# The Fourier gate of a hybrid encoder by Strassen's seven products

## The chip, the cores and the metric

The kernel runs on one core of a Trainium2 chip. The metric is device time of one execution in microseconds (us). The engines are TensorE (PE, matrix products and transposes), VectorE (DVE), ScalarE (ACT), GpSimd (POOL) and SyncE (SP); all data between HBM and SBUF moves by DMAs, which SP, ACT or POOL issue from their own instruction queues. Each engine takes its instructions in order.

## The reference, cut to what matters

Two token streams, 2048 prompt tokens and 512 sample tokens of 1024 channels, go through an attention layer, a Fourier layer and a final RMSNorm. Only the Fourier layer is touched:

```python
def fourier_layer(x, g, w_gate, w_out):
    h = rmsnorm(x, g)
    hg = h.astype(jnp.float32).reshape(b, s, N_FGROUPS, FGROUP_CH)   # 4 groups of 256 channels
    f = jnp.fft.fftn(hg, axes=(1, 3), norm="ortho").real.reshape(b, s, d)
    gate = h @ w_gate                                                # (tokens, 1024) @ (1024, 1024)
    return x + (f * jax.nn.silu(gate)) @ w_out
```

The gate product `h @ w_gate` is what the change rewrites.

## The kernel before, in words

The 2560 tokens are 20 tiles of 128: tiles 0 to 15 of the prompt and 16 to 19 of the sample. Every fp32 product is made as three fp32r matmuls by `matmul3` (L80): high part by high, high by low, low by high. So every operand is first split: ACT casts it to the high part, DVE (or POOL) subtracts that from the source for the low part.

`attention_phase` does the attention layer and writes its result to HBM as `x1d`. Its last out-projection is left over as a list of steps, `tail`. `fourier_phase(tail)` (L560) runs those steps with its own first work laid between them.

The Fourier layer runs in two stages. In the first, each token tile is loaded and normalised (`norm_T` L620: DMA of `x` L623, Square with a sum on ACT L617, L76 on DVE, a power on POOL L77, the scaling on DVE L625), transposed by PE in two halves of four 128x128 blocks (L602), and split (`split_T` L595: ACT L608, DVE L609). From the transposed halves come two products. `channel_dft` (L628) makes z, the DFT along the channels: 24 matmuls of 128x256. `gate` (L641) makes the gate: two output halves, each 8 blocks of the contraction by three matmuls, 48 of 128x512 to a tile; then tanh on ACT (L647), the product on DVE (L648) and a store to `s2d`. `w_gate` is loaded once by `load_res` (L576) in eight steps of 512 KB (`w32g`) and held, split, in 16 tiles of `wres`.

The tiles run in five groups: the sample's four, then the prompt's tiles a, a+4, a+8, a+12 for a = 0 to 3. After each group `radix4` (L655) makes sums and differences of its four z tiles on DVE; for the prompt the odd parts go to HBM (`odd`) and the even parts stay in SBUF. The norm of a tile is issued one tile ahead, and the gate of a tile lags z by one tile, in the last group by three (`pend`). So at the end three gates are left (`last_gates`); they run half by half after the first `position` work, and `load_res` of `w_fout` follows, in the tiles that the gate's weights leave.

In the second stage `position` (L714) makes the DFT along the tokens, multiplies with the gate from `s2d`, and `finish` (L766) makes the out-projection (`fo`), the residual and the final norm.

At the seam of the two phases the loop L674 to L707 matters: `tail` holds the steps of the last out-projection (`op`, residual `xr` added on DVE L475, stored to `x1d`); norms of tiles 16 and 17 are issued after steps 4 and 6, with their loads on ACT's queue, and a step of `load_res` follows each step from the third on. The order within each engine is then made by the framework's scheduler from this program order and the dependencies; buffers in pools of fixed size (here `wres` 16, `x` 3, `s2` 3, `Z` 14, `xr` 3, `hT` 8, PSUM `bank` 6 and `acc` 2) make a writer wait until the former tenant is read.

Of the kernel before, what the change touches and what calls it, by code (L numbers as in the profile page):

```python
# [18 lines left out]
P = 128  # L19
# [12 lines left out]
LINE = 512  # L32
LATE = (0, 8, 9, 10, 11, 12)
# [9 lines left out]
def encoder(  # L43
# [36 lines left out]
    def matmul3(out, a, b, start, stop, w=None):  # L80

        PE.matmul(out, a[0], b[0], start=start, stop=False)  # L82
        PE.matmul(out, a[0], b[1], start=False, stop=False)  # L83
        PE.matmul(out, a[1], b[0], start=False, stop=stop)  # L84
# [475 lines left out]
    def fourier_phase(tail):  # L560
        with ExitStack() as es:
# [4 lines left out]
            SP.dma_start(gb, bass.AP(g1.tensor, g1.offset, [[0, P], [1, D]]))  # L566

            mir = fp.tile([P, 120], I32, name="mir")[:, :8]
            SP.dma_start(mir, mirror)
            ch = fp.tile([P, 2, 2, 256], F32R, tag="tab", bufs=2, name="chan_sb")  # L570
            POOL.dma_start(ch, chan)

            def zt(name):
                return zp.tile([P, D], F32, tag="Z", bufs=14, name=name)

            def load_res(w, name, stage):  # L576

                res, steps = [], []

                def load(half, k2):  # L580
                    w32 = stage(f"w32{name}{half}_{k2}")
                    SP.dma_start(w32, w[half, k2])
                    for kk in range(2):
                        t = fp.tile([P, 2, 512], F32R, align_bytes=LINE, tag="wres", bufs=16, name=f"wr{name}{half}_{k2}_{kk}")
# [35 lines left out]
            def norm_T(t, queue=SP):  # L620

                xt = fp.tile([P, D], F32, tag="x", bufs=3, name=f"x1_{t}")
                queue.dma_start(xt, x1d[t * P : (t + 1) * P, :])  # L623
                inv = sumsq(xt, f"b{t}")
                DVE.scalar_tensor_tensor(xt, xt, inv[:, 0:1], gb, ALU.mult, ALU.mult)  # L625
                return split_T(xt, f"b{t}")

            def channel_dft(t, hT, zscale):  # L628
                z = zt(f"z{t}")
                for hf in range(2):  # L630
                    ps = bank(f"z{t}_{hf}")
                    for gg in range(2):
                        for kk in range(2):
                            matmul3(
                                ps[:, gg * 256 : gg * 256 + 256], hT[hf * 4 + gg * 2 + kk],
                                (ch[:, kk, 0], ch[:, kk, 1]), kk == 0, kk == 1,
                            )
                    ACT.activation(z[:, hf * 512 : hf * 512 + 512], ps, AF.Copy, scale=zscale)
                return z

            def gate(t, hT, halves=(0, 1)):  # L641
                for half in halves:
                    ps = psum2.tile([P, 512], F32, tag="acc", name=f"gp{t}_{half}")
                    for k in range(KD):
                        matmul3(ps, hT[k], wg[half * KD + k], k == 0, k == KD - 1)
                    th = main.tile([P, 512], F32, tag="xr", bufs=3, name=f"gt{t}_{half}")
                    ACT.activation(th, ps, AF.Tanh, scale=0.5)  # L647
                    DVE.scalar_tensor_tensor(th, th, 1.0, ps, ALU.add, ALU.mult)  # L648
# [6 lines left out]
            def radix4(z, name):  # L655

                e, f = zt(f"e{name}"), zt(f"f{name}")
                tt(e, z[0], z[2], ALU.add)
                tt(z[0], z[0], z[2], ALU.subtract)
                tt(f, z[1], z[3], ALU.add)  # L660
                tt(z[1], z[1], z[3], ALU.subtract)
                w2 = zt(f"w{name}")
                tt(w2, e, f, ALU.subtract)
                tt(e, e, f, ALU.add)
                return e, w2, z[0], z[1]


            def s2_tile(name):
                return fp.tile([P, D], F32, tag="s2", bufs=3, name=name)

            def x_tile(name):
                return fp.tile([P, D], F32, tag="x", bufs=3, name=name)
# [41 lines left out]
            def position(name, tab, gr, gs, tiles):  # L714
# [11 lines left out]
                tb = fp.tile([P, 6, P], F32R, tag="tab", bufs=2, name=f"tb{name}")  # L726
# [4 lines left out]
                us = [zp.tile([P, D], F32, tag="u", bufs=2, name=f"u{name}_{i}") for i in range(len(tiles))]  # L731
# [34 lines left out]
            def finish(uT, r, last=False):  # L766
# [3 lines left out]
                if last:  # L770
                    ss = main.tile([P, 8], F32, tag="ss", bufs=2, name="ssl")
                    junk = fp.tile([P, D], BF16, tag="junk", bufs=1, name="jkl")
                x2 = fp.tile([P, D], F32, tag="x", bufs=3, name=f"x2_{r0}")
# [27 lines left out]
            last_gates, pend = pend, []  # L801
# [30 lines left out]
            w0, w2 = ([parts[a][i] for a in range(4)] for i in range(2))  # L832
# [158 lines left out]
```

## Time and profile before

| | |
|---|---|
| time, median of 3 runs | 1725.6 us (1723.79 to 1727.31) |
| profiled execution | 1727.91 us, span 1726.1 us, mean granted clock 0.989 |
| PE busy | 1681.3 us, 97% of the span |
| PE weight loads | 1442.8 us, 84% |
| DVE, ACT, POOL busy | 1119.8, 811.2 and 308.0 us |
| DMA | 306.92 MB, 178 GB/s on average |

The attention phase takes up to about 1124 us of the span, the Fourier layer's first stage (with the last half of the out-projection) from there to about 1452, the second stage the rest. Times in a timeline count from the span's start. A matmul is pipelined: its shown duration overlaps that of the next, so the distance between starts is what one costs. `[2.42 <-DVE x L625]` behind a line is idle time of that engine before the instruction and what ended it.

### The profile page before, as it was taken

The numbers are of one execution on the slowest core, as the hardware profiler recorded it, in microseconds if no ns is written. First come the engines' busy times: TensorE is split into PE (matmuls) and PEld (weight loads), VectorE is DVE, ScalarE is ACT, GpSimd is POOL, SyncE is SP. The second block draws the span as 40 slices with busy tenths as digits, with TensorE's granted clock in tenths as the row PEclk, the third lists the DMA queues.
The fourth block names the chain that finished last, engine by engine and source line by source line (L and its number), as shares of the span: only waits on it lengthen the run. The fifth ranks groups of instructions, "written<-read, shape, count | busy, mean of one in ns | idle before, by whom it ended". The sixth has DMA issues, their size and how long they took to land. (4 is left out here: it accounts for less than half of the span.)

```text
span 1726.1 us, 25388 instructions
## 1 busy us (share of the span) xinstructions
PE 1681.3 (97%) x9100; PEld 1442.8 (84%) x9100; DVE 1119.8 (65%) x2696; ACT 811.2 (47%) x1864; POOL 308.0 (18%) x395
## 2 busy tenths in 40 slices
PE   9999899999989999899999999989999999999998
PEld 7878778888888888888888888878888888888886
DVE  5898655888438885378874688655344348597553
ACT  6677524676226664256652466443332224343221
POOL 2467640111301112101121011100000000011100
PEclk9999899999999999999999999999999999999999
DMA  8478775444574454743538534484322347443421
GB/s 298 165 284 322 265 277 183 160 172 167 201 253 138 155 183 159 269 156 135 203 121 285 209 125 141 144 285 136 108 89 94 109 138 262 161 141 120 143 95 62
DMA packets 83450, 306.92 MB, mean 178 GB/s; under 512 B 9931, under 2 KB 20171, under 8 KB 65404
## 3 DMA queue, kind: packets, MB, share of 16 engines
q1 hardware_dynamic: 75836, 265.18, 45.0%
q0 software_dynamic: 7056, 38.80, 5.7%
q8 instruction: 73, 1.20, 0.3%
q10 hardware_dynamic: 432, 1.31, 0.3%
q14 instruction: 53, 0.43, 0.1%
HBM read 238.11 MB, written 67.14 MB: 177 GB/s over the span
## 5 line engine op out<-in xcount | busy, mean ns | idle before, releaser
L400 ACT ACTIVATE S<-S 128x385 f32<-128x385 f32 (+1 forms) x320 | 191.2, 598 | 53.7 <-DVE S L396 52.7
L417 ACT CAST pts<-pt 128x384 fp32r<-128x384 f32 (+1 forms) x320 | 144.8, 454 | 117.7 <-PE pt L416 113.0
L418 DVE TENSOR_TENSOR pts<-pt,pts 128x384 fp32r<-128x384 f32 (+1 forms) x320 | 168.5, 527 | 42.6 <-ACT pts L417 39.8
L396 DVE CUSTOM_DVE_ANT_0 S<-spt,b 128x385 f32<-128x385 f32 (+1 forms) x320 | 168.8, 528 | 34.2 <-PE spt L384 29.1
L445 POOL TENSOR_TENSOR o<-o,s 128x256 f32<-128x256 f32 x75 | 55.4, 739 | 692.7 <-DVE o L441 686.3
L384 PE MATMUL spt<-kwin,qab 128*128 128x384 f32 (+1 forms) x640 | 159.1, 330 | 8.9 <-DVE S L396 8.9
L405 DVE TENSOR_SCALAR S<-S 128x384 f32<-128x384 f32 (+1 forms) x320 | 149.4, 467 | 9.1
L416 PE MATMUL pt<-ident,S 128*128 128x128 f32 x896 | 150.7, 274 | 0.6 <-DVE pts L418 0.4
L384 PEld LDWEIGHTS spt<-kwin,qab 128*128 128x128 f32 x640 | 118.6, 189 | 37.9 <-DVE S L396 12.6
L82 PE MATMUL gp<-h,wg 128*128 128x512 f32 x320 | 137.7, 430 | 0.0
L82 PE MATMUL qp<-h,wq 128*128 128x512 f32 x320 | 137.1, 429 | 0.6 <-ACT wq L96 0.6
L430 PEld LDWEIGHTS av<-pts,v 128*128 128x128 f32 x896 | 126.6, 190 | 11.5 <-DVE pts L418 0.2
L430 PE MATMUL av<-pts,v 128*128 128x256 f32 x896 | 135.2, 285 | 0.0
L82 PE MATMUL op<-wo,uT 128*128 128x512 f32 x320 | 127.6, 401 | 3.5 <-DVE xr L475 2.8
L416 PEld LDWEIGHTS pt<-ident,S 128*128 128x128 f32 x896 | 114.2, 141 | 16.1 <-DVE pts L418 4.3
L83 PE MATMUL op<-wo,uT 128*128 128x512 f32 x320 | 127.1, 397 | 0.0
L84 PE MATMUL op<-wo,uT 128*128 128x512 f32 x320 | 126.4, 396 | 0.0
L84 PE MATMUL qp<-h,wq 128*128 128x512 f32 x320 | 126.1, 394 | 0.1
L84 PE MATMUL gp<-h,wg 128*128 128x512 f32 x320 | 126.0, 394 | 0.0
L83 PE MATMUL qp<-h,wq 128*128 128x512 f32 x320 | 125.6, 393 | 0.0
L82 PE MATMUL fo<-wrf,tTu 128*128 128x512 f32 x320 | 125.6, 392 | 0.0
L83 PE MATMUL gp<-h,wg 128*128 128x512 f32 x320 | 125.5, 392 | 0.0
(270 smaller groups left out, 3941.7 us busy)
## 6 DMA issues: line engine op xcount, KB each, us to landing
wq<-wsd SPq DMA_DIRECT2D x32, 1024.0 KB, 4.9
wg<-wsd SPq DMA_DIRECT2D x32, 1024.0 KB, 6.7
wo<-wsd SPq DMA_DIRECT2D x32, 1024.0 KB, 4.9
x<-x1d SPq DMA_DIRECT2D x38, 512.0 KB, 3.9
b<-rowd SPq DMA_DIRECT2D x40, 384.0 KB, 4.2
xs<-in_x_dram SPq DMA_DIRECT2D x23, 512.0 KB, 7.4
xr<-in_x_dram SPq DMA_DIRECT2D x40, 256.0 KB, 5.5
x1d<-xr SPq DMA_DIRECT2D x40, 256.0 KB, 4.0
```

The source lines that it names most:

```text
L82: PE.matmul(out, a[0], b[0], start=start, stop=False)
L83: PE.matmul(out, a[0], b[1], start=False, stop=False)
L84: PE.matmul(out, a[1], b[0], start=False, stop=stop)
L384: PE.matmul(ps[:, 2 + k0 * P : 2 + k1 * P], q, kwin[g][:, part, b * P + k0 * P : b * P + k1 * P], start=part == 0, stop=part == 1,)
L396: DVE.tensor_tensor_reduce(out=s[:, e0:e1], in0=ps[:, 1 + e0 : 1 + e1], in1=st["bias"][:, j, 386 - e1 : 386 - e0][:, ::-1], scale=1.0, sca ...
L400: last_exp[0] = ACT.activation(s[:, e0:e1], s[:, e0:e1], AF.Exp, bias=mn, scale=-1.0, accum_out=den)
L405: DVE.tensor_scalar(s[:, ks], s[:, ks], den, None, ALU.mult)
L416: PE.transpose(ps[:, kb, :], s[:, 1 + kb * P : 1 + (kb + 1) * P], ident)
L417: ACT.copy(hi[:, k0:k1, j, :], ps[:, k0:k1, :])
L418: DVE.tensor_tensor(lo[:, k0:k1, j, :], ps[:, k0:k1, :], f32(hi[:, k0:k1, j, :]), ALU.subtract)
L430: PE.matmul(out, v, pt[:, kb].rearrange("p h q -> p (h q)"), start=kb == k0 and part == 0, stop=kb == k1 - 1 and part == 1,)
L445: eng.tensor_tensor(of, of, res["s"][:, cs], ALU.mult)
```

## The change

The gate product now takes two token tiles at once, as a 2 by 2 block product: the rows of A are the two tiles (0 and 1), its columns the halves of the contraction, and B is `w_gate` in quadrants. Strassen's algorithm, in Winograd's form, needs seven products of blocks instead of eight:

- sums of A: S1 = A21 + A22, S2 = S1 - A11, S3 = A11 - A21, S4 = A12 - S2, made on DVE (with ACT copies) from the transposed halves in PSUM for each pair and split like any operand (`sums`, `parts`);
- sums of B: T1 = B12 - B11, T2 = B22 - T1, T3 = B22 - B12, N4 = B21 - T2, made once and split (`build1`, `build2`);
- products: W = A11 B11, X = A12 B21, Z = S1 T1, W += S2 T2, Z += S4 B22, W += S3 T3, W += A22 N4, with ACT and DVE taking W and Z out of PSUM in between; C11 = A11 B11 + X, C12 and C22 are sums of such copies, C21 is the last W.

Each product is 4 blocks by three matmuls of 128x512, so a pair takes 84 instead of 96. Six weight sets (B11, T1, T2, B22, T3, N4) are held in SBUF; the split B21 is written to HBM (`b21d`) and loaded again for each pair in four DMAs of 512 KB on SP. `build1(k)` is laid between the tail's steps where `load_res` was; `build2(k)` reads `w_gate` a second time, after pair 0's transposes. The work of the next pair (transposes, sums, z, and the radix-4 sums of every second pair) is laid between the products by hooks. The pools become two: `L` with 24 slots of 4 KB to a partition, and `R` with 16, which hold almost everything, so that `c`, `x`, `s2`, staged weights and sums share slots. The scratch of Square moves to the three `xr` buffers, which silu tiles and the out-projection's residuals also use. The even parts of `radix4` go to HBM (`evd`) and come back before the second stage's prompt part. At the end the last pair's gates run whole, with `position` of the sample laid in after the first product, and `w_fout` is loaded after them.

In the changed file lines 80 to 560 are shifted by one: L602 of before answers to L662 there, L625 to L639, L609 to L665.

```diff
+def left(shape, dtype, name):
+    return fp.tile(shape, dtype, align_bytes=LINE, tag="L", bufs=24, name=name)
+def right(shape, dtype, name):
+    return zp.tile(shape, dtype, align_bytes=LINE, tag="R", bufs=16, name=name)
+ch = left([P, 2, 2, 256], F32R, "chan_sb")
...
+def split(t, src, lo_engine=DVE):
+    ACT.copy(t[:, 0], src)
+    lo_engine.tensor_tensor(t[:, 1], src, f32(t[:, 0]), ALU.subtract)
+    return t[:, 0], t[:, 1]
...
-    junk = fp.tile([P, D], BF16, tag="junk", bufs=1, name=f"jk{name}")
+    junk = main.tile([P, 512], F32, tag="xr", bufs=3, name=f"jk{name}").bitcast(BF16)
     ACT.activation(junk, src, AF.Square, accum_out=ss[:, 0:1])
     return inv_rms(ss, 1, f"inv{name}")
...
+class Pair:
+    def __init__(self, n, ts):
+        self.n, self.ts, self.x, self.ps, self.A, self.F, self.S = n, ts, [None, None], {}, {}, {}, {}
+        self.zs = [None, None]
+    def norms(self, i, queue=SP):
+        self.x[i] = norm(self.ts[i], queue)
+    def turn(self, i, hf):
+        name = f"b{self.ts[i]}_{hf}"
+        ps = bank(f"tr{name}")
+        for k in range(4):
+            c0 = (hf * 4 + k) * P
+            PE.transpose(ps[:, k * P : (k + 1) * P], self.x[i][:, c0 : c0 + P], ident)
+        t = main.tile([P, 2, 512], F32R, align_bytes=LINE, tag="hT", bufs=8, name=f"tT{name}")
+        ACT.copy(t[:, 0], ps)
+        DVE.tensor_tensor(t[:, 1], ps, f32(t[:, 0]), ALU.subtract)
+        self.ps[i, hf], self.A[i, hf] = ps, (t[:, 0], t[:, 1])
+    def sums(self, i):
+        ps, F = self.ps, self.F
+        if i in (1, 4):
+            self.pair = left([P, 2, 512], F32, f"s{i}_{self.n}")
+        out = F[i] = self.pair[:, i in (2, 3)]
+        if i % 2:
+            ACT.copy(out, ps[1, 0])
+        a, b, op = {
+            1: lambda: (out, ps[1, 1], ALU.add),
+            2: lambda: (F[1], ps[0, 0], ALU.subtract),
+            3: lambda: (ps[0, 0], out, ALU.subtract),
+            4: lambda: (ps[0, 1], F[2], ALU.subtract),
+        }[i]()
+        DVE.tensor_tensor(out, a, b, op)
+    def parts(self, i):
+        self.S[i] = split(left([P, 2, 512], F32R, f"S{i}_{self.n}"), self.F[i])
...
+def prod(out, a, b, ks, first):
+    for k in ks:
+        cs = slice(k * P, (k + 1) * P)
+        matmul3(out, (a[0][:, cs], a[1][:, cs]), b[k], first and k == 0, k == 3, not first)
+def gates(pr, hooks):
+    n, A, S = pr.n, pr.A, pr.S
+    W = psum2.tile([P, 512], F32, tag="acc", name=f"W{n}")
+    Z = psum2.tile([P, 512], F32, tag="acc", name=f"Z{n}")
+    X = bank(f"X{n}")
+    b21 = []
+    def more():
+        if len(b21) < 4:
+            t = right([P, 2, 512], F32R, f"b21_{n}_{len(b21)}")
+            SP.dma_start(f32(t), f32(b21d[len(b21)]))
+            b21.append((t[:, 0], t[:, 1]))
+    def x_step(k):
+        prod(X, A[0, 1], b21, (k,), True)
+        more()
+    def silu(c, i, half):
+        th = main.tile([P, 512], F32, tag="xr", bufs=3, name=f"gt{pr.ts[i]}_{half}")
+        ACT.activation(th, c, AF.Tanh, scale=0.5)
+        DVE.scalar_tensor_tensor(th, th, 1.0, c, ALU.add, ALU.mult)
+        t = pr.ts[i]
         dst, t0 = (s2d[0], t) if t < SEQ // P else (s2d[1], t - SEQ // P)
         SP.dma_start(dst[t0 * P : (t0 + 1) * P, half * 512 : half * 512 + 512], th)
+    def hook(i):
+        for h in hooks.get(i, ()):
+            h()
+    more()
+    more()
+    four = range(4)
+    c = left([P, 2, 512], F32, f"c{n}")
+    c11, c22 = c[:, 0], c[:, 1]
+    prod(W, A[0, 0], wg["B11"], four, True)
+    ACT.copy(c11, W)
+    hook(0)
+    x_step(0)
+    prod(Z, S[1], wg["T1"], four, True)
+    ACT.copy(c22, Z)
+    hook(1)
+    prod(W, S[2], wg["T2"], four, False)
+    c12 = fp.tile([P, 512], F32, tag="c12", bufs=1, name=f"c12_{n}")
+    ACT.copy(c12, W)
+    hook(2)
+    x_step(1)
+    prod(Z, S[4], wg["B22"], four, False)
+    DVE.tensor_tensor(c12, c12, Z, ALU.add)
+    silu(c12, 0, 1)
+    hook(3)
+    x_step(2)
+    prod(W, S[3], wg["T3"], four, False)
+    DVE.tensor_tensor(c22, c22, W, ALU.add)
+    silu(c22, 1, 1)
+    hook(4)
+    x_step(3)
+    DVE.tensor_tensor(c11, c11, X, ALU.add)
+    silu(c11, 0, 0)
+    hook(5)
+    prod(W, A[1, 1], wg["N4"], four, False)
+    silu(W, 1, 0)
+    hook(6)
+b21d = [dram.tile([P, 2, 512], F32R, name=f"b21d{k}") for k in range(4)]
+wg = {w: [None] * 4 for w in ("B11", "T1", "T2", "B22", "T3", "N4")}
+def stage_w(w, k, name):
+    rows = []
+    for r in (k, k + 4):
+        t = left([P, 2, 512], F32, f"w32{name}{r}")
+        SP.dma_start(t, w[:, r // 2, :, (r % 2) * 512 : (r % 2) * 512 + 512].rearrange("h p c -> p h c"))
+        rows.append(t)
+    return rows[0][:, 0], rows[0][:, 1], rows[1][:, 0], rows[1][:, 1]
+def build1(k):
+    def w(name):
+        return left([P, 2, 512], F32R, f"w{name}_{k}")
+    b11, b12, b21, b22 = stage_w(w_gate, k, "g")
+    wg["B11"][k] = split(w("B11"), b11)
+    DVE.tensor_tensor(b12, b12, b11, ALU.subtract)
+    wg["T1"][k] = split(w("T1"), b12)
+    DVE.tensor_tensor(b11, b22, b12, ALU.subtract)
+    wg["T2"][k] = split(w("T2"), b11)
+    wg["B22"][k] = split(w("B22"), b22, POOL)
+    t = w("B21")
+    split(t, b21, POOL)
+    POOL.dma_start(f32(b21d[k]), f32(t))
+def build2(k):
+    def w(name):
+        return right([P, 2, 512], F32R, f"w{name}_{k}")
+    b11, b12, b21, b22 = stage_w(w_gate, k, "h")
+    DVE.tensor_tensor(b22, b22, b12, ALU.subtract)
+    DVE.tensor_tensor(b21, b21, b11, ALU.subtract)
+    DVE.tensor_tensor(b21, b21, b22, ALU.subtract)
+    wg["T3"][k] = split(w("T3"), b22)
+    wg["N4"][k] = split(w("N4"), b21, POOL)
...
 order = [[16, 17, 18, 19]] + [[a, a + 4, a + 8, a + 12] for a in range(4)]
-ahead = []
-wg, loads = load_res(w_gate, "g", s2_tile)
+pairs = [Pair(2 * gi + i // 2, tiles[i : i + 2]) for gi, tiles in enumerate(order) for i in (0, 2)]
+builds = [lambda k=k: build1(k) for k in range(4)]
 for i, s in enumerate(tail):
     s()
     if i in (4, 6):
-        ahead.append(norm_T(order[0][len(ahead)], ACT))
-    if i >= 2 and loads:
-        loads.pop(0)()
-for s in loads:
-    s()
+        pairs[0].norms((i - 4) // 2, ACT)
+    if i % 2 and builds:
+        builds.pop(0)()
 wstack.close()
 zp = es.enter_context(tc.tile_pool(name="zp", bufs=1, side="right", reuse_waits="tile"))
-todo = [t for tiles in order for t in tiles][2:]
-parts = []
-pend = []
-for gi, tiles in enumerate(order):
-    zs = []
-    for t in tiles:
-        hT = ahead.pop(0)
-        if todo:
-            ahead.append(norm_T(todo.pop(0)))
-        zs.append(channel_dft(t, hT, 1.0 if gi == 0 else 0.5))
-        pend.append((t, hT))
-        if len(pend) > (3 if gi == 4 else 1):
-            gate(*pend.pop(0))
-    r = radix4(zs, f"r{gi}")
-    if gi == 0:
-        for i in range(4):
-            SP.dma_start(gsd[i], r[i])
-    else:
-        parts.append(r[:2])
-        for i in range(2):
-            SP.dma_start(odd[gi - 1, i], r[2 + i])
+def turns1(pr):
+    pr.turn(1, 0)
+    pr.turn(1, 1)
+    pr.sums(1)
+def turns2(pr):
+    pr.turn(0, 0)
+    pr.sums(2)
+    pr.parts(1)
+    pr.turn(0, 1)
+    pr.sums(4)
+    pr.parts(2)
+def turns3(pr):
+    pr.parts(4)
+def turns4(pr):
+    pr.sums(3)
+    pr.parts(3)
+def combine(pr):
+    if pr.n % 2 == 0:
+        return
+    gi = pr.n // 2
+    r = radix4(pairs[pr.n - 1].zs + pr.zs, f"r{gi}")
+    for i in range(4):
+        SP.dma_start(gsd[i] if gi == 0 else evd[gi - 1, i] if i < 2 else odd[gi - 1, i - 2], r[i])
+evd = dram.tile([4, 2, P, D], F32, name="evd")
+pr = pairs[0]
+for f in (turns1, turns2, turns3, turns4):
+    f(pr)
+build2(0)
+build2(1)
+for i, hf in HALVES:
+    pr.z(i, hf)
+build2(2)
+build2(3)
+for n, pr in enumerate(pairs[:-1]):
+    nx = pairs[n + 1]
+    for i in range(2):
+        nx.norms(1 - i)
+    gates(pr, {
+        1: [lambda: turns1(nx)], 2: [lambda: turns2(nx)], 3: [lambda: turns3(nx)], 4: [lambda: turns4(nx)],
+        5: [lambda: nx.z(1, 0), lambda: nx.z(1, 1)],
+        6: [lambda: nx.z(0, 0), lambda: nx.z(0, 1), lambda: combine(nx)],
+    })
...
-first = position(*sample(1, (2, 3)))
-for half in range(2):
-    for t, hT in last_gates:
-        gate(t, hT, (half,))
+first = []
+gates(pairs[-1], {0: [lambda: first.extend(position(*sample(1, (2, 3))))]})
...
-w0, w2 = ([parts[a][i] for a in range(4)] for i in range(2))
+w0, w2 = [], []
+for i, l in enumerate((w0, w2)):
+    for a in range(4):
+        t = zt(f"ev{a}_{i}")
+        SP.dma_start(t, evd[a, i])
+        l.append(t)
```

More of the change, by code (lines that the diff above doesn't have):

```diff
@@ L32 @@
 LINE = 512
+HALVES = ((1, 0), (1, 1), (0, 0), (0, 1))
 LATE = (0, 8, 9, 10, 11, 12)
@@ L78, in inv_rms, with matmul3 @@
         return inv
[L80 to L84, printed above, removed]
+    def matmul3(out, a, b, start, stop, more=False):
+        PE.matmul(out, a[0], b[0], start=start, stop=False, skip_group_check=more)
+        PE.matmul(out, a[0], b[1], start=False, stop=False, skip_group_check=more)
+        PE.matmul(out, a[1], b[0], start=False, stop=stop, skip_group_check=more)
     def load_w(c, n, name, lo_engine=None, late=None):
@@ L583, in load @@
                     for kk in range(2):
-                        t = fp.tile([P, 2, 512], F32R, align_bytes=LINE, tag="wres", bufs=16, name=f"wr{name}{half}_{k2}_{kk}")
+                        t = left([P, 2, 512], F32R, f"wr{name}{half}_{k2}_{kk}")
                         src = w32[:, kk * 512 : kk * 512 + 512]
@@ L615, in sumsq, with norm @@
                 ss = main.tile([P, 8], F32, tag="ss", bufs=2, name=f"ss{name}")
-                junk = fp.tile([P, D], BF16, tag="junk", bufs=1, name=f"jk{name}")
+                junk = main.tile([P, 512], F32, tag="xr", bufs=3, name=f"jk{name}").bitcast(BF16)
                 ACT.activation(junk, src, AF.Square, accum_out=ss[:, 0:1])
                 return inv_rms(ss, 1, f"inv{name}")
-            def norm_T(t, queue=SP):
-                xt = fp.tile([P, D], F32, tag="x", bufs=3, name=f"x1_{t}")
+            def norm(t, queue=SP):
+                xt = left([P, D], F32, f"x1_{t}")
                 queue.dma_start(xt, x1d[t * P : (t + 1) * P, :])
@@ L625, in norm_T, with z @@
                 DVE.scalar_tensor_tensor(xt, xt, inv[:, 0:1], gb, ALU.mult, ALU.mult)
[L626 to L630, printed above, removed]
+                return xt
+            class Pair:
[30 more added lines that the diff above has]
+                    self.S[i] = split(left([P, 2, 512], F32R, f"S{i}_{self.n}"), self.F[i])
+                def z(self, i, hf):
+                    t = self.ts[i]
+                    if hf == 0:
+                        self.zs[i] = zt(f"z{t}")
@@ L637, in channel_dft @@
                             )
[L638 to L648, printed above, removed]
+                    ACT.activation(
+                        self.zs[i][:, hf * 512 : hf * 512 + 512], ps, AF.Copy, scale=1.0 if t >= SEQ // P else 0.5
+                    )
@@ L725, in position @@
                     s2s.append(s2)
-                tb = fp.tile([P, 6, P], F32R, tag="tab", bufs=2, name=f"tb{name}")
+                tb = left([P, 6, P], F32R, f"tb{name}")
                 POOL.dma_start(tb.rearrange("p a c -> p (a c)"), tabs[tab])
@@ L730, in position @@
                 asb = main.tile([P, 4, P], F32, tag="xr", bufs=3, name=f"as{name}")
-                us = [zp.tile([P, D], F32, tag="u", bufs=2, name=f"u{name}_{i}") for i in range(len(tiles))]
+                us = [zt(f"u{name}_{i}") for i in range(len(tiles))]
                 for hf in range(2):
```

30 lines of the change are left out of this document (15 added, 15 removed).

## The prediction

> **What bounds the kernel now.** I read the page's first lines, then a table of stretches across the stage that is changed, the waits of TensorE (PE) where the stage begins, PE's timeline there, and last the rows by shape that price what is added.
>
> ```profile
> span 1726.1 us, 25388 instructions
> PE 1681.3 (97%) x9100; PEld 1442.8 (84%) x9100; DVE 1119.8 (65%) x2696; ACT 811.2 (47%) x1864; POOL 308.0 (18%) x395
> ```
>
> PE is busy for 97% of the span, so the kernel ends when PE's work ends. All times below are of this one profiled execution, 1727.91 us (span 1726.1, and 1.8 around it); it lies 2.3 above the median of 1725.6 and 0.6 above the highest of the three runs. About 0.2% (3.5 us) is what a measurement of this kernel can tell from no change.
>
> ```profile
> 1123.00:1165.00 42.00, 36.67 (x166) 29.90 (x166) 24.05 (x39) 18.26 (x33) 2.20 (x4) 0.92 0.85 291
> 1165.00:1200.00 35.00, 35.00 (x205) 30.93 (x204) 19.98 (x27) 14.49 (x27) 3.55 (x5) 0.99 0.39 125
> 1200.00:1260.00 60.00, 60.00 (x328) 51.98 (x327) 23.12 (x31) 18.04 (x32) 4.18 (x5) 1.00 0.38 125
> 1400.00:1460.00 60.00, 57.93 (x289) 48.22 (x289) 49.60 (x66) 25.87 (x50) 1.14 (x2) 1.00 0.67 221
> ```
>
> Columns: stretch, its length, busy time of PE, its weight loads, DVE, ACT, POOL, then granted clock, DMA share, GB/s. From 1165 to 1400 PE never stands still while DVE needs 38% and ACT 30%: each matmul taken out there shortens the kernel by its whole length. The first row is the opposite: at the start of the stage PE stands for 5.3 us at a clock of 0.92, and DMA is at 85%.
>
> ```profile
> PE trb L602 <- DVE x L625: 4.7, 2, 2.4
> PE op L82 <- DMA wo<-wsd: 0.6, 1, 0.6
> ...
> 1157.61 0.39 PE L82 MATMUL gp<-wrg,tTb 128*128 128x512 f32 x1
> 1157.83 0.39 PE L83 MATMUL gp<-wrg,tTb 128*128 128x512 f32 x1
> 1160.64 1.06 PE L602 MATMUL trb<-ident,x 128*128 128x128 f32 x8 [2.42 <-DVE x L625]
> 1162.25 0.41 PE L84 MATMUL z<-chan_sb,tTb 128*128 128x256 f32 x1
> 1162.47 0.41 PE L82 MATMUL z<-chan_sb,tTb 128*128 128x256 f32 x1
> ```
>
> The first two lines are PE's waits from 1123 to 1200, the others its timeline. The stage starts thinly: PE waits for the norm (L625) ahead of its transposes. Gate matmuls follow each other every 0.2266 us (12 in 2.72).
>
> **The change, part by part.**
>
> 1. *Matmuls removed.* A pair of token tiles took 2 x 48 gate matmuls and takes 7 products of 12 = 84. Ten pairs lose 120 x 0.2266 = **-27.2 us**. z (128x256 at 0.12, 24 per tile, 2.88) and transposes (0.8 per tile) stay. A pair falls from 29.1 to 26.4 us of PE. The extra copies and sums per pair, priced by the rows L609 (0.683), L653 (1.22), L625 (1.283) on DVE and 0.6 for ACT's casts, make DVE about 19 us (24 with the radix-4 sums that every second pair carries) and ACT 15, both under 26.4, so PE hides them. If that cover goes, see rival C. DMA per pair is b21 2 MB, x 1 MB, s2d 1 MB, radix results about 1 MB on average: 5 MB in 26.4 us, 190 GB/s, more than the 91 to 125 of now and less than the 291 that the first row carried.
>
> 2. *The start, until PE gets its first pair.* The last half of the out-projection takes 96 x 0.2266 = 21.75 us and begins at 1122.97, as now. Before, 28 gate matmuls of tile 16 and tile 16's transposes stood between it and the norms; x_16 was fetched on ACT's queue at 1122.58 and squared at 1128.37. In the changed order that fetch stands on ACT behind the copies of build1(0) and build1(1), and the first work of PE after the out-projection is the transposes of x_17, behind build1(2) too. The chain: w32g_1 is issued on SP behind a store and a wo load, and lands at about 1140.5 (w32g's first cast ran 7.3 after its issue, 1134.40 against 1127.06); a build is five 128x512 copies on ACT alternating with five DVE operations, 4.4 us; fetch of x_16, with ACT standing for it, 5 (3.9 on SP, 6.8 on ACT); Square 1.06 + 0.19, L76 0.15, POOL's pow 0.55, L625 1.28; the rest of build1(2) 3.75; fetch of x_17, 4.8; and 3.4 again for its norm. 1140.5 + 4.4 + 5 + 3.4 + 3.75 + 4.8 + 3.4 = 1165.3. Bounds 1162.5 (both fetches 3.9, less on the loads) and 1172 (both 6.8, and a late w32g). PE ends its out-projection at 1122.97 + 21.75 + 0.6 = 1145.3 and stands for **20 us**. Queued behind ACT's stand are the hi copies, and DVE waits for those.
>
> 3. *The start, pair 0.* From 1165.3 DVE works off what queued: lo halves of builds 2 and 3, the sums, and four out-projection residuals whose loads now share the three "xr" buffers with the Square's scratch. The z banks wait for the third and fourth of them, to about 1177.5; the S parts are there at 1181.5; PE is through the first two products by 1184.5, with 13.5 us of work in 19. Then W·T2 waits for the copy of W. Its tile c takes a left slot that frees only when build2(3) has made its sums, and build2's loads are let through two or three slots at a time: the pairs of w32h land at about 1179, 1189.4, 1193.5 and 1198. So the copy comes at about 1199.5; b21_0, issued on SP behind x_19 and x_18, lands at 1202.4, and the norms of 19 and 18 are done at 1203.4 and 1205.4. PE stands for another 15 to 18 us. What is left of PE's work (X0 to X3 2.7, B22, T3 and N4 8.2, four transposes 1.6, z of 18 and 19 5.8) is 18.3, so pair 0 and these z end at 1203.4 + 18.3 + 1 = **1222.7**. Before, z(19) and gates 16 and 17 ended at 1192.3 with 0.8 of tile 0's transposes done too: **+31.2**, of which 2.7 of saved matmuls are already taken off. Bounds: +22 (1162.5, staging through one slot more) and +40.
>
> 4. *b21, reloaded for each pair.* In pairs 2, 4, 6 and 8 X0 follows W·B11 directly, 5.6 after the pair before ends, while b21_0's load stands on SP behind that pair's last silu store (1.85 after the end) and takes 3.9 to 5.1: 0.15 to 1.35 each, taken as 0.8, **+3.2** (0 to 6). In odd pairs X0 follows Z·T1, 8.1 after, and nothing waits.
>
> 5. *The end of the stage.* Before, the last three gates run half by half (16 us of PE) while w_fout is cast; the row of 1400 to 1460 shows 2.1 us of idle. Now the last pair has no z or transposes of a next one between products; N4 waits 0.8 for the c22 sum; w32f's loads stand on SP behind the silu stores and need freed slots, and DVE's queue delays the lo part of the first transposed tile. By the same chaining the first final tile ends 42.5 us after the pair begins, with 34.4 of work: 8 against 2.1, **+6.0** (3 to 9).
>
> 6. *Small ones.* evd's 8 stores and 8 loads of 512 KB (4 MB each way, SP) are issued early enough to lie beside the final stage; their cover is the sample steps ahead of emit(0, 8), and were it gone 4 MB at 150 GB/s would be some 27 us. I take 0 (0 to 3). Clock: in the timeline one stand of 2.42 us is followed by 16 z matmuls at 0.213 for 0.12, 1.6 us. Of the two long stands most of that falls on work that waits for DVE anyway: **+1**.
>
> The Trainium skill, "TensorE: Matmul & The Clock Gate" (Part 1 and "Why this matters for your kernels"), puts the gap that halves the clock at about 3 us and the way back at about 3.4 us of work. The trace agrees with the second (1161.9 to 1165.2) and shows a stand of 2.42 us that already did it. By the rule (an estimate from that page) each stand above 3 us costs some 1.7 us in full, which for six of them would put the sum about 9 us higher, still inside the forecast's own range; the 0.8 us waits of step 4 would cost nothing more.
>
> **Sum** against the span: pair 0 +31.2; nine further pairs 9 x 12 x 0.2266 = -24.5; b21 +3.2; end +6.0; clock +1; tile 0's 0.8 is in the first. +16.9 us, 1727.9 + 16.9 = **1744.8**; against the median, 2.3 lower. I say 1744.
>
> **Rivals.**
>
> *B, faster: the build does not hold PE in pair 0.* If slots free early enough, step 3 vanishes: from 1165.3 PE needs 1.6 + 5.8 + 19 + 1.6 + 5.8 = 33.8 and ends at 1199.1, +7.6 instead of +31.2. Sum 16.9 - 23.6 = -6.7, **1721**. For it: DVE is busy for 24 of 42 us and ACT for 18 there, POOL for 2, so no engine is short of time; against: DMA at 85%, and that W's copy needs a slot of the last build. It decides where pair 0 ends before about 1206.
>
> *C, slower still: pairs with the radix-4 sums become bound by DVE or slots.* The sum for c22 is done about 22.7 us into such a pair and N4 needs it at 24: 1.3 us of margin, in a queue with six 1.22 us sums. 2 to 3 us late in five pairs adds 10 to 15: **1757**. For it: the buffers L and R are full and x waits for slots; against: a DVE load of 24 in 26.4 still fits.
>
> *D, all waits hidden:* 27.2 less, **1700**. Only if the start costs what it does now; the chain of step 2 speaks against it.
>
> *E, the fetches of step 2 and the slots of step 3 at half my price:* +16.9 - 15 = +2, **1729**, within the measurement.
>
> **How the numbers follow.** Forecast (1731 to 1758 as its own range) 0.57, C 0.17, B 0.15, D 0.05, E 0.06. Faster: B and D, with a third of E, 0.22; same: half of E and the low edge of the forecast, 0.04; slower 0.74. The range reaches to B's middle and a little over C: 1717 to 1763, which leaves out D and the outer parts of B and C. The number is the forecast's, 1744.
>
> **What would show it.** Step 1: 120 fewer 128x512 matmuls, and pairs 26.4 to 27.5 us apart from about 1225 to 1435. Step 2: a PE stand of about 20 us from 1145, ended by the norm of x_17 (L639). Step 3: a stand of 15 us or so ahead of W·T2 or X0, ended by ACT's copy of W or by b21's DMA; pair 0 done at 1222. Step 4: short waits X <- DMA b in even pairs. Step 5: 8 us idle around the last pair and the first final tile. What makes it wrong: w32g landing well before 1140, x fetched in less than 4, or PE waiting for DVE's c22 in the radix-4 pairs.

## The result, and the profile after

The changed kernel takes 1751.15 us (median of four runs, 1746.94 to 1751.57) against 1725.92 us before: a ratio of 1.0142, with a 95% interval of 1.0123 to 1.0161. It is slower by about 25 us, though it has 120 matmuls less to do. The profiled execution is the fastest of the four, 1746.94 us (span 1745.2); against the profiled execution before it is 19.0 us longer. The page's first lines and TensorE's row:

```profile
span 1745.2 us, 25593 instructions
PE 1663.0 (95%) x8980; PEld 1422.9 (82%) x8980; DVE 1204.3 (69%) x2826; ACT 865.3 (50%) x1966; POOL 323.6 (19%) x411
```

PE is busy 18.3 us less and idle 37.4 us more (82.2 against 44.8). The table of stretches (the same columns as before) says where:

```profile
1123.00:1165.00 42.00, 25.43 (x118) 21.01 (x117) 22.72 (x33) 16.05 (x29) 14.48 (x14) 0.80 0.73 261
1165.00:1200.00 35.00, 18.42 (x100) 15.54 (x98) 24.76 (x35) 17.16 (x32) 6.86 (x7) 0.76 0.67 235
1200.00:1230.00 30.00, 30.00 (x164) 25.99 (x163) 22.10 (x31) 14.31 (x26) 1.08 (x2) 1.00 0.55 192
1440.00:1480.00 40.00, 33.92 (x152) 27.18 (x151) 30.69 (x49) 20.23 (x40) 1.05 (x2) 0.91 0.93 333
```

From 1123 to 1200 PE stands for 33 of 77 us. From 1200 to 1230 it is full again; later come short waits, and another 6 us stand open around 1460. PE's waits, first from 1120 to 1230, then from 1230 to 1436 and from 1436 to 1490:

```profile
PE trb L662 <- DVE x L639: 16.4, 2, 16.1
PE W L83 <- ACT c L746: 16.3, 1, 16.3
...
PE X L83 <- DMA b<-b21d: 5.7, 6, 2.2
...
PE tru L616 <- DVE us L948: 3.3, 2, 1.9
PE fo L85 <- DVE tTu L623: 3.2, 1, 3.2
...
```

Two long waits and a handful of short ones make nearly all of it. In PE's timeline the two long ones look so (`...` stands for rows left out, here and below); the last two lines are where two pairs begin, 28.0 us apart because the first of them waits 1.08 us for b21:

```profile
1158.45 1.97 PE L662 MATMUL trb<-ident,x 128*128 128x128 f32 x8 [16.13 <-DVE x L639]
...
1190.50 0.79 PE L83 MATMUL W<-wT,S 128*128 128x512 f32 x1 [16.28 <-ACT c L746]
...
1298.26 0.40 PE L83 MATMUL W<-wB,tTb 128*128 128x512 f32 x1
...
1326.27 0.40 PE L83 MATMUL W<-wB,tTb 128*128 128x512 f32 x1
```

What fed the two waits is in ACT's timeline: the first row is the first copy of w_gate's second block; then the fetch of x_16, its Square (4.5 us of standing), the fetch of x_17 and its Square, and last the copy of W into tile c. That copy comes directly behind the cast of the last T3 block of `build2`, which itself waited for DVE's sum; so it stood behind `build2` in ACT's order as well as for a slot, and the trace doesn't separate the two.

```profile
1137.39 0.62 ACT L586 CAST wB<-w32g 128x512 fp32r<-128x512 f32 x1 [3.57 <-DMA w32g<-in_w_gate_dram]
...
1140.11 0.34 ACTq L637 DMA_DIRECT2D x<-x1d  x1
...
1146.30 1.06 ACT L631 ACTIVATE jkb<-x 128x1024 bf16<-128x1024 f32 x1 [4.54 <-DMA x<-x1d]
...
1151.45 0.33 ACTq L637 DMA_DIRECT2D x<-x1d  x1
...
1154.79 1.06 ACT L631 ACTIVATE jkb<-x 128x1024 bf16<-128x1024 f32 x1 [1.69 <-DMA x<-x1d]
...
1189.14 0.62 ACT L586 CAST wT<-w32h 128x512 fp32r<-128x512 f32 x1 [1.92 <-DVE w32h L806]
1189.86 0.58 ACT L746 COPY c<-W 128x512 f32<-128x512 f32 x1
```

The attention phase, whose code is the same, ended at slightly different times in the profiled executions (its last `av` matmuls start at 1119.16 before, 1116.89 after, and at 1117 to 1122 in the experiments), so stages are compared from that point on:

| from the last `av` matmuls, us | before | after | difference |
|---|---|---|---|
| gates 16, 17 and z 16 to 19 done | 73.2 | 96.8 | +23.6 |
| first transposes of the final stage | 332.5 | 344.5 | +12.0 |
| end of the span | 606.9 | 628.3 | +21.4 |

By the first landmark, before has also transposed two further tiles, 0 and 4 (1.6 us). So the start costs 25.2 us like for like, the stretch of the pairs gives back 13.1, and the passage into the final stage costs 9.3. The attention's earlier end in this execution takes 2.3 off.

### The profile page after: what moved, and what is told of

The parts are those of the page before. It is cut to its first block, busy times and chain, and to the rows that moved or that the text cites. A ratio compares the mean times of both kernels' runs of the same rounds, so it can differ in the third digit from the quotient of the medians.

```text
span 1745.2 us, 25593 instructions
## 1 busy us (share of the span) xinstructions
PE 1663.0 (95%) x8980; PEld 1422.9 (82%) x8980; DVE 1204.3 (69%) x2826; ACT 865.3 (50%) x1966; POOL 323.6 (19%) x411
## 4 chain that ended last, share of the span: by engine, by line
PE 72%; DVE 12%; DMA 8%; issue 4%; ACT 3%; POOL 2%; SPq 1%; DVEq 0%; POOLq 0%; ACTq 0%
PE av L431 5%; PE spt L385 5%; PE pt L417 5%; PE qp L85 4%; PE qp L83 4%; PE qp L84 4%; PE gp L83 3%; PE gp L85 3%; PE gp L84 3%; PE op L83 3%; PE op L85 3%; PE op L84 3%; PE fo L85 3%; PE fo L83 3%; PE fo L84 3%
## 5 line engine op out<-in xcount | busy, mean ns | idle before, releaser
L83 PE MATMUL gp<-h,wg 128*128 128x512 f32 x320 | 137.7, 430 | 0.0
L83 PE MATMUL qp<-h,wq 128*128 128x512 f32 x320 | 137.1, 429 | 0.6 <-ACT wq L97 0.6
L85 PE MATMUL fo<-wrf,tTu 128*128 128x512 f32 x320 | 126.2, 394 | 3.2 <-DVE tTu L623 3.2
L83 PE MATMUL fo<-wrf,tTu 128*128 128x512 f32 x320 | 126.9, 396 | 0.0
L85 PE MATMUL qp<-h,wq 128*128 128x512 f32 x320 | 126.2, 394 | 0.1
L85 PE MATMUL gp<-h,wg 128*128 128x512 f32 x320 | 125.9, 393 | 0.0
L84 PE MATMUL fo<-wrf,tTu 128*128 128x512 f32 x320 | 125.8, 393 | 0.0
```

What stands on the lines that cost most here:

```text
L83: PE.matmul(out, a[0], b[0], start=start, stop=False, skip_group_check=more)
L84: PE.matmul(out, a[0], b[1], start=False, stop=False, skip_group_check=more)
L85: PE.matmul(out, a[1], b[0], start=False, stop=stop, skip_group_check=more)
```

## The experiments

The theory was that the start is one chain: the builds, with two fetches in it on ACT, then the second reading of w_gate through a few free slots of pool L; and that PE's saving is had in every pair after that. The rivals were a start bound by the bytes that arrive, engines that are simply behind, and pairs bound by DVE or slots. Ratios are to the kernel before, on the same chip; the changed kernel has 1.0142. "From the last av" means the profiled span from that point, 628.3 for the changed kernel.

**The norms first.**

```diff
+            for i in (1, 0):
+                pairs[0].norms(i)
             for i, s in enumerate(tail):
                 s()
-                if i in (4, 6):
-                    pairs[0].norms((i - 4) // 2, ACT)
```

> The norms of tiles 17 and 16 are issued ahead of the out-projection's steps and of the four first builds, with their loads on SP, instead of between the builds with their loads on ACT. Chain theory (the first stand of 16.1 us is the builds and the two fetches standing one behind the other on ACT): the stand before the transposes of x_17 falls from 16.1 to under 4 us, and as ACT no longer stands for two fetches the builds end some 8 us earlier, so the second stand doesn't take all of it back: 1738 to 1744, 8 to 13 less than the changed kernel. Rival, transfers (the start is bound by the bytes that have to arrive, 8 MB of w_gate among them): the transposes come early but the stand ahead of W.T2 grows by what the first one loses; within 3 us of the changed kernel, 1748 to 1752.

Measured: 1745.42 us, 1.0117 (1.0089 to 1.0145); 626.2 from the last av. PE's waits from 1100 to 1200:

```profile
PE W L83 <- ACT c L746: 15.0, 1, 15.0
PE op L83 <- DVE xr L476: 6.5, 1, 6.5
...
```

The stand before x_17's transposes is gone, yet the next landmark comes only 0.8 us earlier (96.0 against 96.8). Part of the gain went into a new wait of the out-projection, whose residuals now wait for the scratch of the early Squares in the shared xr buffers; the wait for W's copy stays at 15.0. The edit also made the builds later: the last loads of w32g are issued on SP 37 us after the last `av` instead of 20, and the last build's first copy comes at 43.4 instead of 39.0. So this run doesn't price the first stand alone; it shows that the chain theory missed, as the builds didn't end 8 us earlier and the wait for W's copy stayed. The time alone would fit the transfer rival, and its interval overlaps that of the changed kernel; the next experiment names the holder of the second stand.

**No second reading.** T3 and N4 are replaced by sets that are there (`wg["T3"][k] = wg["T2"][k]`, `wg["N4"][k] = wg["B22"][k]`) and the rest of `build2` is taken out.

> The second reading of w_gate is left out with its sums and splits: the products with T3 and N4 take the sets T2 and B22 instead, so the gate's C21 and C22 are not computed. Slot theory (the stand of 16.3 us ahead of W.T2 is pair 0's tile c waiting for a slot of the staged second reading, which comes through two or three slots): this stand goes, 12 to 18 us less than the changed kernel, 1733 to 1739, with the stand before x_17 unchanged at 16. Rival, engines' backlog (DVE and ACT are behind with the first builds and the residuals, and W's copy would be late anyway): under 6 us less, 1745 to 1751.

Measured: 1732.33 us, 1.0048 (1.0035 to 1.0060); 610.5 from the last av, 17.8 less than the changed kernel. PE's waits at the start:

```profile
PE trb L662 <- DVE x L639: 16.0, 2, 15.5
...
```

The wait for W's copy is gone whole, with the first stand as before. So `build2` sets the end of pair 0: pair 1 starts 15.8 us earlier (81.0 after the last `av`). This run removes its reading, sums and splits together, and does not say which.

**Reading once.** `build1` computes T2 in b12's place, then T3 = T2 - B11 and N4 = B21 - T2 into the staged tile, and `build2` only splits them, for all k ahead of pair 0's transposes:

```diff
-                DVE.tensor_tensor(b11, b22, b12, ALU.subtract)
-                wg["T2"][k] = split(w("T2"), b11)
+                DVE.tensor_tensor(b12, b22, b12, ALU.subtract)
+                wg["T2"][k] = split(w("T2"), b12)
+                DVE.tensor_tensor(b11, b12, b11, ALU.subtract)
...
+                DVE.tensor_tensor(b12, b21, b12, ALU.subtract)
+                kept.append((b11, b12))
...
-                b11, b12, b21, b22 = stage_w(w_gate, k, "h")
...
+                t3, n4 = kept[k]
+                wg["T3"][k] = split(w("T3"), t3)
+                wg["N4"][k] = split(w("N4"), n4, POOL)
```

> w_gate is read once: the first builds leave T3 = T2 - B11 and N4 = B21 - T2 in the staged tile, and these are split into their sets right behind the out-projection, ahead of pair 0's transposes. Slot theory (the stand ahead of W.T2 is the staged second reading): that stand goes as where the second reading was left out, but eight more copies and splits (5 us of ACT, 5 of DVE) stand before pair 0's own, so 8 to 15 us less than the changed kernel: 1.0055 to 1.0095 of before, against 1.0142. Rival (the stand is not the reading but the sums, copies and splits on ACT and DVE, which are all still there): 0 to 4 less, 1.012 to 1.014.

Measured: 1738.28 us, 1.0094 (1.0062 to 1.0127); 616.4 from the last av, 11.9 less. Its PE timeline shows one long stand and then pair 1:

```profile
1163.55 4.00 PE L662 MATMUL trb<-ident,x 128*128 128x128 f32 x16 [19.30 <-DVE x L639]
...
1206.28 0.40 PE L83 MATMUL W<-wB,tTb 128*128 128x512 f32 x1
```

That is two thirds of the 17.8 us; at the start of pair 1 (87.5 after the last `av`) it is 9.3 of 15.8. So the second reading, with the slots it needs, is worth more than half. The rest is put down to the sums and splits that remain, but this run also moves the splits ahead of the transposes (the first stand grows from 16.1 to 19.3), and no run separates the two.

> The same, and the norms of tiles 17 and 16 ahead of the builds with loads on SP. With the second reading gone nothing is left to take back what the early norms gain: by the chain theory pair 0 is ready when the builds are, and the early norms take two fetches (10 us) and two norms (7 us) out of the chain on ACT: 6 to 12 us less than the same kernel with late norms, 1.000 to 1.005 of before. Rival (early norms only move the stand, as they did with the second reading in place, where they gave 2 us): within 3 us of the same kernel with late norms.

With the norms early as well (the first diff on top): 1733.83 us, 1.0052 (1.0036 to 1.0068), 613.3 from the last av. The gain over late norms is 3.1 us by the profiled spans, 4.5 by the medians and 0.42% (some 7 us) by the ratios, whose intervals overlap; so it is not settled whether the 6 to 12 expected were reached. PE now waits 5.7 us for a residual, 8.6 for high parts of x that stand behind weight copies on ACT, and 2.3 for a copy of z.

**The steady pairs.** One product more per pair (`prod(Z, S[1], wg["T1"], four, True)` twice):

> The product S1 T1 is made twice in each pair, the second time over the first: 12 more matmuls of 128x512 in each of the ten pairs, nothing else. If PE bounds the pairs, as the timeline shows for all but pair 0 and the waits for b21, nine pairs take 2.72 us more each and pair 0 and the last little or all of it: 22 to 27 us more, 1773 to 1778. Rival (DVE or the slots of L and R set the pace of the radix-4 pairs, so PE's saving isn't had there): half of the pairs hide it, 10 to 15 us more.

Measured: 1768.36 us, 1.0250 (1.0222 to 1.0279), 22.8 more from the last av. Pairs that wait for nothing are 29.36 us apart instead of 26.63, so 2.73 for 12 matmuls. The pairs with the radix-4 sums on DVE are among these; the four others still wait for b21, 4.0 us in all. So PE bounds every pair that doesn't wait for b21, and rival C of the prediction falls.

b21 on another queue (`POOL.dma_start` for `SP.dma_start` in `more`):

> The four loads of b21 per pair are issued on POOL instead of SP. Queue theory (X0 waits in the even pairs because the load stands on SP behind the last silu store of the pair before, and X3 in pair 1 for a like reason): the waits X <- DMA b, 5.7 us, go, and the slow matmuls behind the 2.2 us one with them: 5 to 7 us less, 1744 to 1746. Rival (b's buffers of pool R come free too late, or POOL's transfers land later than SP's): no change or slower, 1749 to 1760.

Measured: 1750.95 us, 1.0162 (1.0132 to 1.0192). The pairs do what the queue theory says: eight of them take 215.2 us instead of 222.2. But the span from the last av is only 1.1 less. Of the 7.0, 1.9 were lost before pair 1, 0.8 at w_fout's casts (fo waits 3.5 for ACT's wrf), and 3.2 behind PE's last matmul, whose last row begins 11.4 us before the span ends instead of 8.2. The last stores are issued and landed no later after it; what holds the end there stays open.

b21 earlier on the same queue: the first two loads for the next pair are issued right behind `x_step(3)`.

```diff
                 x_step(3)
+                if n + 1 < len(pairs):
+                    for _ in range(2):
+                        more(n + 1, pairs[n + 1].b21)
```

> The first two loads of b21 for the next pair are issued right behind the last product that reads this pair's b21, ahead of two silu stores on SP, not behind them; still on SP. Queue theory: the waits X <- DMA b, 5.7 us, go as on POOL (eight pairs in 215.2 us instead of 222.2) and nothing is given back later: 6 to 8 us less than the changed kernel, 1.0095 to 1.0108 of before. Rival (what POOL's queue gave back came from the pairs ending sooner, because w_fout or the radix-4 results are late then): 0 to 3 less.

Measured: 1741.49 us, 1.0106 (1.0068 to 1.0145); 619.7 from the last av, 8.6 less. All of PE's waits from 1230 to 1436, and the beginnings of pairs 2 and 3:

```profile
PE W L83 <- DVE c L765: 0.3, 1, 0.3
...
1243.88 0.40 PE L83 MATMUL W<-wB,tTb 128*128 128x512 f32 x1
...
1270.51 0.40 PE L83 MATMUL W<-wB,tTb 128*128 128x512 f32 x1
```

From pair 2 on every pair is 26.63 apart, and the eight take 213.6 us instead of 222.2: the place of the load in SP's queue was the whole of step 4. By the ratios the gain is 0.36%, some 6 us. Pair 1 still takes 27.22; it has the one wait that is left, 0.3 us for the sum of c22, the wait that rival C priced at 2 to 3 us.

**The clock.** 64 matmuls into a spare bank (`warm`), meant for each stand.

> 64 matmuls of 128x512 into a spare bank are laid into each of the two long stands of the changed kernel (64 x 0.2266 = 14.5 us of the 16.1 and 16.3), ahead of the transposes of x_17 and behind Z.T1 of pair 0; nobody reads the bank. Clock theory (the stands cost more than their length, as PE's clock is halved behind them: transposes at 1.97 instead of 1.03, W.T2 at 0.79 a matmul shown): the slow rows go and pair 0 ends 2 to 4 us earlier, 0.1 to 0.2% less than the changed kernel. Rival (slow matmuls lie beside a wait of DVE that ends at the same time anyway): no change, and the stand ahead of W.T2 is longer by what the transposes gain.

Measured: 1763.77 us, 1.0238 (1.0206 to 1.0269). Only half of the theory was tested. The scheduler put the second group behind W·T2, where PE was not waiting, and there it cost about its length: pair 1 starts 112.8 after the last av instead of 96.8. The first group stood where it should; its last stretch, and what follows:

```profile
1155.77 2.88 PE L880 MATMUL warm<-chan_sb 128*128 128x512 f32 x12
1160.63 1.50 PE L662 MATMUL trb<-ident,x 128*128 128x128 f32 x8 [1.99 <-DVE x L639]
1163.04 1.97 PE L662 MATMUL trb<-ident,x 128*128 128x128 f32 x8 [0.90 <-DVE xr L476]
```

Two microseconds of rest were enough for slow transposes, and W·T2 came no earlier (74.3 after the last av against 73.6). For the second stand the theory wasn't tested.

**The end.** Six of w_fout's eight loads with their casts as hooks of the last pair (`3: loads[:2], 4: loads[2:4], 5: loads[4:6]`):

> Six of the eight loads and casts of w_fout are laid between the last pair's products (two each after the second, third and fourth of its hooks) instead of all behind it. Slot and queue theory of the end (the 3.2 us before the first fo, and part of the slow clock behind it, come from w32f's loads that stand behind the last silu stores and from DVE's queue): the waits fo <- DVE tTu and tru <- DVE us shrink, 2 to 6 us less than the changed kernel, 1.011 to 1.013 of before. Rival (the casts now stand ahead of the silu work on ACT and DVE, which are in order, so that N4 and the sums wait for w32f's landing): the same or up to 6 us more, 1.014 to 1.018.

Measured: 1749.81 us, 1.0137 (1.0111 to 1.0162): no difference. The wait for tTu falls from 3.2 to 0.8, but fo then waits 2.9 for the casts of w_fout and the clock drops there instead. The theory missed: an earlier place in the program did not make the casts of the weights come early enough.

**All together, and what is left of the start.** Reading once, early norms and early b21 loads:

> w_gate read once, norms of 17 and 16 ahead of the builds, and the first two b21 loads of the next pair ahead of the silu stores. If the three gains add (5 + 4 + 6 us of 0.48%, 0.42% and 0.36% as each was measured alone), 0.9985 to 1.003 of before: level with it. If they overlap (b21 waits in the first pairs are those of a start that is too fast for them), 1.003 to 1.006.

Measured: 1725.34 us, 1.0002 (0.9989 to 1.0016): level with before, as three gains that add. The stretches at the start (columns as above):

```profile
1120.00:1145.00 25.00, 19.60 (x77) 15.04 (x76) 11.77 (x18) 6.19 (x11) 4.69 (x5) 0.86 0.79 262
1145.00:1165.00 20.00, 11.39 (x57) 9.29 (x55) 19.13 (x23) 11.44 (x21) 11.35 (x9) 0.83 0.86 303
```

Now DVE is busy for 19.1 of 20 us while PE stands for 8.6. Two more kernels went for this. The first moves the early Squares' scratch into c12, lays the late splits between pair 0's own and gives T3's low part to POOL:

> The same, with three orders changed at the start: the Square scratch of tiles 17 and 16 in the c12 tile instead of the residuals' xr buffers, the splits of T3 and N4 laid between pair 0's own splits instead of ahead of its transposes, and T3's low part on POOL instead of DVE. Theory (what is left of the start is PE's 5.7 us wait for a residual that waits for a scratch buffer, and 8.6 us for hi parts that stand behind eight weight copies on ACT): both go and pair 0 ends 6 to 12 us earlier, 0.994 to 1.000 of before, so faster than before by up to 0.6%. Rival (the builds on DVE and ACT are the bound whatever their order): within 3 us of the kernel without these three.

Measured: 1726.31 us, 1.0004 (0.9990 to 1.0017). The waits changed places (4.5 for S, 7.7 for wB, 2.5 for S's low part) and pair 1 starts 84.3 after the last av, against 83.0. The second also stages the lower half of each w_gate block, and B21, in the idle hT buffers:

> As the kernel with the three orders changed at the start, and the lower half of each staged w_gate block and the split B21 on its way to HBM are held in the eight hT buffers (idle between the attention's last chunk and pair 0's transposes) instead of in slots of L, so that the staging of a build doesn't wait for slots of the one before; half of the reading and B21's part can also start earlier, beside the attention. Slot theory (the builds are 9 to 10 us apart, because w32g of builds 2 and 3 is only issued at 1149 and 1153 us when slots come free): the builds move together, PE's waits for wB and S in pair 0 (14.7 us) shrink by half or more: 6 to 12 us less, 0.993 to 0.997 of before. Rival (DVE, which is busy for 18 to 19 of 20 us from 1145 to 1165, is the bound of the builds): 0 to 4 us less, 0.998 to 1.0005 of before.

Measured: 1726.60 us, 1.0009 (0.9994 to 1.0023). Pair 1 starts 79.3 after the last av, 5.0 earlier, and the waits for wB and S shrink from 14.7 to 8.2, so slots did space the builds. But the last av itself comes 2.8 later in the span: B21's early copies run beside the attention's last chunk, where ACT stands 3.3 us for a staged block, DVE waits behind ACT and PE 2.6 us for DVE. So 2.2 us of the 5.0 are left, and no difference shows in the time. Both theories missed their forecasts. Their rival, the engines' work itself (DVE is busy for 17.7 to 19.1 of the 20 us from 1145 in these three kernels), is what the traces leave, but no run tests it; no run here beat the kernel before.

## Why the prediction was right or wrong

The direction, the range and the mechanism held. The forecast was 18 us above the median, and it came out at 25; by the profiled executions 17 was forecast and 19 came. That the second pair lies so close is partly luck: the start cost 6.0 less than forecast, b21 5.4 and the end with its clock about 5 more, and the attention's earlier end took 2.3 off. The terms:

1. *Matmuls removed, -24.5 in nine pairs.* This held. The first z matmuls of two tiles start 29.32 apart before (1189.44 and 1218.76) where nothing waits, and a pair takes 26.63 after; the prediction's 29.1 and 26.4 are both 0.2 too low. The difference of 2.69 gives 24.2 in nine pairs. That DVE and ACT stay covered held: an added product cost its full 2.73, and the only wait for a sum is the 0.3 us above.
2. *The first stand, 20 us.* It measured 16.1, ended by the norm of x_17 as forecast. From the first copy of the second block to the transposes it took 21.1 us, where the sum had 24.8. Two terms were too large: the rest of build1(2) runs beside the norm's DVE and POOL part (x_17's fetch is issued 5.2 after x_16's Square, not 7.2), and x_17's fetch held ACT for 3.3, not 4.8.
3. *Pair 0, a second stand of 15 to 18 us.* It measured 16.3, at the forecast place with the forecast releaser, ACT's copy of W. Leaving `build2` out removed it; reading w_gate once gained two thirds as much by the span's end. Like for like the start costs 25.2 against 31.2 predicted, inside its bounds. (The prediction counted the transposes of only one of the two further tiles, 0.8.) What the two steps did not see is that the first stand can't be taken away alone: early norms gained 2 us, because the residuals then wait for the scratch and the builds come later.
4. *b21, +3.2.* The four even pairs gave 0.32, 1.08, 0.41 and 1.45, together 3.3. The step missed X3 of pair 1, 2.2 us, with 1.6 us of slow matmuls behind it; with early loads the whole step was worth 8.6 in the trace.
5. *The end, +6.0.* Too small. Waits of 0.8, 0.6, 1.5, 3.2 and 1.9 us, and 3.0 us of slow fo matmuls behind the 3.2, make about 11, against 2.1 of waits before. The passage to the final stage was priced to the first fo tile only. What the other terms leave of the 21.4 is 11.8, clock included, against 7.0 forecast; not all of it was found.
6. *evd at nothing, clock +1.* No wait for evd appears in any stage. At the start the clock cost no more than before (4 to 5 us of slow matmuls in both kernels); behind X3 and the first fo it cost some 4.6, so the term was mis-sized. The estimate from the Trainium skill, "TensorE: Matmul & The Clock Gate", put the sum 9 higher and counted six stands above 3 us; three came (16.1, 16.3 and 3.2), and the wait at X3 that cost 1.6 was one of 2.2.

Rival B needed pair 0 done by 1206 (1203.7 with this execution's earlier attention); it ended at 1213.7.

## What to carry to other kernels

An algorithm that saves work in a full steady state has to be charged for its set-up in the stage where the busiest engine is already waiting: here 24 us of saved matmuls met 25 us at the start and 20 at b21 and the end. Count what the set-up reads twice, which buffers its staging shares with the first tile, and where its loads stand in an in-order queue. Where two stands lie one behind the other, leave out the cause of each to see what it is worth before changing an order: moving the norms forward made residuals and builds later, and gained 2 us of a stand of 16.

## What the runs showed that was not expected

A rest of about 2 us can slow the matmuls behind it, but doesn't always. Behind waits of 1.88, 1.96, 2.23 and 2.42 us (in the kernels with the eighth product, with w_fout early, after and before) PE ran for 3.3 to 3.4 us at some 0.21 us per 128x256 instead of 0.12, or as much slower per 128x512, and lost 1.4 to 1.7 us. Behind waits of 1.32 to 1.45, and behind one of 1.86 and one of 2.57, it lost 0.1 to 0.2. The slow stretch begins 0.3 to 1.3 us after the restart. In these rows of the changed kernel the first z matmuls are still at full speed:

```profile
1233.55 0.50 PE L83 MATMUL X<-b,tTb 128*128 128x512 f32 x1 [2.23 <-DMA b<-b21d]
...
1234.36 0.28 PE L83 MATMUL z<-chan_sb,tTb 128*128 128x256 f32 x1
1234.47 0.37 PE L84 MATMUL z<-chan_sb,tTb 128*128 128x256 f32 x1
...
1237.85 0.32 PE L85 MATMUL z<-chan_sb,tTb 128*128 128x256 f32 x1
```

One wait shows the chance best. The second transposes of the final stage wait 1.85 to 1.87 us in the changed kernel and in all twelve experiments. In six of these thirteen traces the fo matmuls behind them run at full speed, in seven at half. First the changed kernel, then the one with early b21 loads:

```profile
1485.84 0.63 PE L616 MATMUL tru<-ident,us 128*128 128x128 f32 x4 [1.85 <-DVE us L948]
1487.35 0.39 PE L84 MATMUL fo<-wrf,tTu 128*128 128x512 f32 x1
...
1477.38 0.63 PE L616 MATMUL tru<-ident,us 128*128 128x128 f32 x4 [1.86 <-DVE us L953]
1479.11 0.63 PE L84 MATMUL fo<-wrf,tTu 128*128 128x512 f32 x1
```

The Trainium skill, "TensorE: Matmul & The Clock Gate" (Part 1), says that the activity window runs free of the program, so that the same code meets it at another phase. The thirteen traces fit that. The bound of about 3 us for a harmless gap, in the same page of the Trainium skill ("Why this matters for your kernels"), does not fit the slow stretches behind rests of 1.86 to 2.42 us.
